# The first three up chunks split during the out-projections, and chunk 5 by seven products

## The chip, the cores and the metric

The kernel runs as one program on 1 core of a Trainium2 chip. The metric is the device time of one execution in microseconds; the median of the runs is compared. The profile is of one execution of its own.

## The reference

A trunk of two residual layers on x of 512 tokens by 1024 features, float32. Layer 0 mixes tokens with a gated linear attention (GLA), layer 1 with grouped-query softmax attention of 8 heads of 128. Each mixer ends with an out-projection, and a gated MLP follows it:

```python
def conv_ffn(h, w_up, w_conv, b_conv, w_down):
    u = h @ w_up                      # 1024 -> 2 x 2816
    u = conv(u) + b_conv              # width 3 along the tokens, per feature
    val, gate = jnp.split(u, 2, axis=-1)
    return (jax.nn.silu(gate) * val) @ w_down

for i in range(DEPTH):
    x = x + mixer_i(rmsnorm(x, norm_mix[i]))       # ends in "@ w_out"
    x = x + conv_ffn(rmsnorm(x, norm_ffn[i]), ...)
```

## The kernel before

**Numbers in two parts.** Each fp32 operand is split into a high part (fp32r, a copy that rounds) and a low part (the rest), and one fp32 product is three fp32r matmuls: high x high, high x low, low x high (`mm3`; L482 to L484 for a tile of 512 tokens). ScalarE makes the high part (L319), VectorE the low part by a subtraction (L320). Instead of that subtraction the low part can be made by a DMA: ScalarE writes the high part (L271) and its negative (L272), and a DMA from POOL's queue adds the full values onto that (`low_dma`, L308), from SBUF or from the weights in DRAM.

**Weights.** `Weights` holds a list of pieces to make, in the order of their use (`todo`). A piece of 128 x 1024 is loaded by SyncE into one of 5 buffers of the tag raw, then made into a high and a low part in buffers of the tags wh and wl (4 each); within the FFN every third piece goes into pairs of the tag x. `piece` makes what is asked for, then makes pieces ahead until the count given is ready, and starts the loads of the next ones. Larger buffers of the tag g (22) hold temporaries of all kinds (`big`).

**The up projection.** The 2816 features of u are 22 chunks of 128, each for val and gate. A chunk is done in one of two ways. The plain way (`plain_up`, L1041) takes two weight pieces of one layout and does 2 halves x 8 k-tiles x 3 = 48 matmuls of 128x512. The other (`seven_up`, L1083) is a scheme of Strassen's kind: seven products of half the size in place of eight, with sums of quarters of the weights (`summed`, L275: L283, L286, L293, L294) and of the inputs (`prepare_input`, L1164: differences of quarters, L1168 to L1171). It does 7 products x 4 pairs x 3 = 84 matmuls of 128x256 (L1074). ScalarE copies partial results between the products (L1095, L1102, L1129), and VectorE adds one pair (L1132). `SEVEN` lists the chunks done so, and the host lays their weights out by quarters. The first product of a chunk of sevens runs between the halves of the chunk before it. Of the pieces of sevens, those in `LOW_0` take the DMA for the low part of their first sum.

After either way come a convolution (L1117 on ScalarE, L1118 and L1119 on VectorE), silu and the product of the two halves (L1121, L1122). From chunk 9 on the down projection runs between up chunks.

**The inputs.** For the chunks 0 to 2 (below `SWITCH`) the matmuls read x times the norm's weight (xhl), and the result is multiplied by the tokens' factor R (L1062). Meanwhile `rescale` (L1029) makes four tiles xr of the fully normalised input, each of two k-tiles (L1035), with high parts nh on ScalarE and low parts nl by DMA; the chunks from 3 on read those. `prepare_input` changes the four xr in place into the differences, and makes the parts xt from them, again with the DMA. `INPUT_AT` says after which chunk this is done for which tile.

**Out-projections.** `out_steps` gives them as steps, each for one k-tile of one group of output features. In layer 0 (GLA) 8 steps run early, and the rest after the last two heads' tails. In layer 1 (attention) the twelve steps of `O_STEPS` run between the last heads' blocks, and the rest at the end. Heads end on TensorE with po (probabilities times v, L482 to L484), which reads pth (L1454, ScalarE) and ptl (L1455, VectorE); then oT is made from po (L1336 on ScalarE, L1337 on VectorE), and the out-projection's op (L535) reads it.

**What sets the order.** Instructions of an engine run in program order, which the scheduler of the language makes from the order of the code, the buffers and the dependencies. The engines meet through semaphores, and each queue of DMAs goes in order.

Of the kernel before, what the change touches and what calls it, by code (L numbers as in the profile page):

```python
# [9 lines left out]
F32R = mybir.dt.float32r  # L10
# [39 lines left out]
OUT_FIRST = 8  # L50
# [8 lines left out]
O_STEPS = (20, 22, 24, 27, 30, 33, 34, 34, 35, 35, 36, 37)  # L59
# [7 lines left out]
DOWN_AFTER = {9: 0, 17: 1}  # L67


SEVEN = (6, 7, 8, 10, 11, 12, 13, 15, 16, 18, 19, 20, 21)  # L70
UPA = 3
PA = 4
LOADS = 3
SWITCH = 3
INPUT_AT = {2: (0, 1), 3: (2,), 4: (3,)}
Q_DMA = ()
UP_DMA = (1, 2, 5)
LOW_0 = (7, 8)
LOW_1 = ()
LOW_2 = ()  # L80
STRIP_0 = ()
# [8 lines left out]
UPAW = 3  # L90
# [10 lines left out]
def hybrid_encoder_kernel(  # L101
# [39 lines left out]
    def bank(tag, n):  # L141
        return pp.tile([P, S], F32, tag=tag, bufs=PS[tag], name=nm(n))

    def pair(tag, bufs, dt, n):
        return sp.tile([P, 2 * S], dt, tag=tag, bufs=bufs, name=nm(n))

    def big(dt, n):
        return pair("g", 22, dt, n)
# [27 lines left out]
    class Weights:  # L176
# [68 lines left out]
        def make(self, key):  # L245
            src, i, h = key
            if i < 0:
                self.made[id(src), i, h] = self.make_vg(src, -i, h)
                return
            self.load(key)  # L250
            if (id(src), i) in self.sums:
                self.made[id(src), i, h] = self.summed(src, i, h)
                return
            r = self.loaded.pop((id(src), i, h))
            hi, lo = self.two()
            if any(src is a and i < n for a, n in self.by_dma):
                self.low_dma(hi, lo, r)
            elif any(src is a and i in UP_DMA for a in up):
                self.low_dma(hi, lo, r, src[i, :, h * 2 * S : (h + 1) * 2 * S].bitcast(F32R))
            else:  # L260
                self.split(hi, lo, r, 2 if src is w_first else 1, src is w_first and i == 0 and h == 0)
            self.made[id(src), i, h] = (hi, lo)
# [12 lines left out]
        def summed(self, src, i, h):  # L275
# [20 lines left out]
            r = self.strip[id(src), i][h]  # L296
            low = (LOW_0, LOW_1, LOW_2) if any(src is a for a in up) else (STRIP_0, (), STRIP_2)
            if i in low[h]:
# [41 lines left out]
    W = Weights()  # L340
    up = [w_up[i] for i in range(2)]
    down_w = [w_down[i] for i in range(2)]

    def add_up(layer, chunks):
        for m in chunks:
            W.add(up[layer], (m,), 4 if m in SEVEN else 2)
            if m in SEVEN and m - 1 not in SEVEN and m - 1 not in DOWN_AFTER:
                W.todo[-5:-3] = W.todo[-4], W.todo[-5]
# [137 lines left out]
    def feature_steps(wh, wl, hl, ps):  # L486

        for k in range(KC):
            sl = slice(k * P, (k + 1) * P)
            last = mm3(ps, wh[:, sl], wl[:, sl], *hl[k], k == 0, k == KC - 1)  # L490
            if k == 2:
                W.flush()
            yield last

    def feature_tile(*a):
        for last in feature_steps(*a):
            pass
        return last
# [20 lines left out]
    def out_steps(src, hl, nxt, late, order=(0, 1)):  # L519
# [20 lines left out]
        def end(ng):  # L540
            for n in range(2):
                c = ng * 2 + n
                dve.tensor_tensor(x[c], x[c], pss[ng][n], ALU.add)
                nxt.chunk(c)
            x_save(ng, order[0])
# [6 lines left out]
        for ng in (2, 3):  # L552
            yield from part(ng, [k for ks in late for k in ks])
            end(ng)


    def gla(norm, nxt):
        norm.high(0)
# [367 lines left out]
        def tail(h, last=None):  # L926

            t3 = gr.pop(h)
            for c in range(2):
                tp = bank("pt", "tp")  # L930
                for s in range(NT):
                    with tc.issue_after(last.ins) if last else ExitStack():
                        pe.transpose(tp[:, s * P : (s + 1) * P].bitcast(F32R),
                                     t3[:, s * DV + c * P : s * DV + (c + 1) * P], identr)
                t = big(F32R, "oT") if h >= 2 else pair("xhl", 8, F32R, "oT")
                w = prm[:, PC_GN + c : PC_GN + c + 1]
                act.activation(t[:, :S], tp, AF.Copy, scale=w)  # L937
                dve.scalar_tensor_tensor(t[:, S:], tp, w, t[:, :S].bitcast(F32), ALU.mult, ALU.subtract)
                oh[2 * h + c] = (t[:, :S], t[:, S:])
# [66 lines left out]
        osteps = out_steps(w_gout, oh, nxt, ((4, 5, 6, 7), (0, 1), (2, 3)), (1, 0))  # L1006
# [2 lines left out]
        sync.dma_start(cw, conv)  # L1009
        tail(0)  # L1010
        tail(1)
        for _ in osteps:
            pass
        return cw


    def ffn(layer, norm, cw, nxt):
        w_dn = down_w[layer]

        ahead = {(m + i // 2, i % 2): n for m in DOWN_AFTER for i, n in ((-1, 2), (0, 2), (1, 5))}  # L1020
        ahead.update({(m - 1 + i // 2, i % 2): n for m in SEVEN for i, n in ((-1, 2), (0, 2), (1, 5))})
        plain = {}
# [4 lines left out]
        scaled, fresh = [], []  # L1027
# [13 lines left out]
        def plain_up(m):  # L1041

            pss = []
            for t in range(2):
                ps = bank("s" if t else "acc", "up")
                feature_tile(*W.half(up[layer], 2 * m + t, max(UPAW if W.wide else UPA, ahead.get((m, t), 1))), norm.hl if m < SWITCH else fresh, ps)
                pss.append(ps)
                if t == 0 and m not in DOWN_AFTER:
                    begin_up(m + 1)
                if t == 0 and m in DOWN_AFTER:  # L1050
                    down.append(down_part(DOWN_AFTER[m], m))
                    next(down[-1])
                if m == 0 and t == 0:
                    norm.tokens()
                elif m == 0:
                    norm.rows()
                    rescale()
            for t, ps in enumerate(pss):
                u = ps
                if m < SWITCH:  # L1060
                    u = tmp("u", "u")
                    dve.tensor_tensor(u, ps, norm.R, ALU.mult)  # L1062
                yield t, u
# [14 lines left out]
        def begin_up(m):  # L1078
            if m in SEVEN:
                begun.append(seven_up(m))  # L1080
# [29 lines left out]
        def act_up(m):  # L1110

            res = {}
            for t, u in begun.pop(0) if m in SEVEN else plain_up(m):
                cc = ((layer * 2 + t) * FC + m) * 4
# [122 lines left out]
        for m in range(FC):  # L1237
# [5 lines left out]
            held.append(act_up(m))  # L1243
            for p in INPUT_AT.get(m, ()):
                prepare_input(p)
# [7 lines left out]
            else:  # L1253
                for i, y in enumerate(held):
                    t = big(F32R, "gu")
# [15 lines left out]
    def attention(norm, nxt):  # L1271
# [67 lines left out]
        def whole(gen):  # L1339
            while True:  # L1340
                try:
                    next(gen)
                except StopIteration as e:
                    return e.value
# [44 lines left out]
        ps = [bank("acc" if j < 2 else "pt", "av") for j in range(NT)]  # L1389
# [81 lines left out]
        osteps = out_steps(w_aout, oh, nxt, (range(5), (5,), (6,), (7,)))  # L1471
# [8 lines left out]
        for t in range(len(blocks) + LAG2):  # L1480
# [12 lines left out]
                turn(h, j // 2)  # L1493
            if 1 <= t <= len(blocks):
                copy(*blocks[t - 1])
        whole(osteps)

    norms = [Norm(i) for i in range(4)]
    cw = gla(norms[0], norms[1])
# [5 lines left out]
def _layout(inputs):  # L1505
# [61 lines left out]
    seven = np.stack(quarters, 1).transpose(0, 4, 3, 1, 2, 5).reshape(2, FC, P, 4 * S)  # L1567
    a["w_up"][:, list(SEVEN)] = seven[:, list(SEVEN)]
    dn = i["ffn_w_down"].reshape(2, FC, P, KC, P)
# [29 lines left out]
```

## Time and profile before

| | |
|---|---|
| median of 3 runs | 1087.22 us (1086.87 to 1087.8) |
| span of the profiled execution | 1085.5 us |
| TensorE busy (matmuls) | 1077.5 us, 99% of the span |
| VectorE busy | 888.5 us, 82% |
| ScalarE busy | 721.1 us, 66% |
| POOL busy | 136.7 us, 13% |
| DMA moved | 164.52 MB, mean 152 GB/s |
| TensorE clock granted | 1.00 throughout the stages named below |

The profile is of one execution with a span of 1085.5 us; the median of the timed runs is 1.7 us above it. Its times count from the start of the span. PE is TensorE, DVE VectorE, ACT ScalarE, SP SyncE. L numbers are lines of the kernel before; in the changed kernel they stand 5 to 10 lines lower. The out-projection of layer 0 ends near 218 us, the one of layer 1 near 736 us, and the FFN starts stand behind these.

### The profile page before, as it was taken

Reading aid. Unit: us, or ns where it says so; the run is one execution under the profiler, and the core shown is the slowest. Engines: PE = TensorE matmul, PEld = TensorE weight load, DVE = VectorE, ACT = ScalarE, POOL = GpSimd, SP = SyncE. Lnnn points to the kernel's source line nnn. Section 1 sums busy time; section 2 is a strip of 40 time slices with the busy share of each in tenths; the row PEclk is TensorE's granted clock in tenths of the full one; section 3 lists DMA queues with packets and bytes.
Section 4 is the critical chain, followed back from the end, with each engine's and each line's share of the span. In section 5 each row is a group of like instructions: output and inputs, shape, how many; then the busy total and the mean of one; then the engine's idle time right before and its main releaser. Section 6 shows DMA issues by size and latency. Waiting matters only on the chain.

```text
span 1085.5 us, 17391 instructions
## 1 busy us (share of the span) xinstructions
PE 1077.5 (99%) x6672; PEld 966.4 (89%) x6672; DVE 888.5 (82%) x1327; ACT 721.1 (66%) x1134; POOL 136.7 (13%) x153
## 2 busy tenths in 40 slices
PE   9999999999999999999999999999999999999998
PEld 8888988888999999999988888888889999999997
DVE  7998967569898899988755588666989889998882
ACT  8679575478775676666574677656877567666660
POOL 0212112021001100010015333002110010001000
PEclk9999999999999999999999999999999999999999
DMA  8744446499545633274767475549863473227542
GB/s 301 187 126 106 122 141 215 154 207 204 127 125 127 145 120 111 77 177 121 252 149 162 127 204 164 164 158 202 206 148 124 105 166 116 100 80 157 136 175 78
DMA packets 55763, 164.52 MB, mean 152 GB/s; under 512 B 6528, under 2 KB 7040, under 8 KB 55680
## 3 DMA queue, kind: packets, MB, share of 16 engines
q1 hardware_dynamic: 36192, 112.66, 32.2%
q0 software_dynamic: 14592, 42.21, 21.7%
q10 hardware_dynamic: 4896, 8.55, 2.1%
q8 instruction: 52, 0.85, 0.3%
q14 instruction: 31, 0.25, 0.1%
HBM read 114.89 MB, written 14.68 MB: 119 GB/s over the span
## 4 chain that ended last, share of the span: by engine, by line
PE 87%; DVE 6%; ACT 3%; DMA 2%; issue 2%; POOL 0%; SPq 0%; DVEq 0%; ACTq 0%; POOLq 0%
PE r L1074 37%; PE op L535 8%; PE vg L652 7%; PE up L482 4%; PE up L483 4%; PE up L484 4%; PE dn L483 2%; PE dn L484 2%; PE dn L482 2%; PE av L509 1%; PE A L482 1%; DVE wl L320 1%; PE A L484 1%; DMA nl<-xr 1%; PE B L484 1%
## 5 line engine op out<-in xcount | busy, mean ns | idle before, releaser
L320 DVE TENSOR_TENSOR wl<-raw,wh 128x1024 fp32r<-128x1024 f32 x156 | 189.8, 1220 | 31.3 <-ACT wh L319 31.1
L319 ACT ACTIVATE wh<-raw 128x1024 fp32r<-128x1024 f32 x156 | 162.6, 1053 | 73.4 <-PE op L535 20.7
L1074 PE MATMUL r<-gu,wh 128*128 128x256 f32 x896 | 161.2, 282 | 0.0
L1074 PE MATMUL r<-xt,wh 128*128 128x256 f32 x832 | 151.1, 283 | 0.4 <-ACT r L1095 0.3
L1074 PEld LDWEIGHTS r<-gu,wh 128*128 128x128 f32 x896 | 139.3, 190 | 1.0 <-ACT r L1211 0.2
L1074 PEld LDWEIGHTS r<-xt,wh 128*128 128x128 f32 x832 | 129.2, 190 | 1.6 <-ACT r L1095 1.1
L1074 PE MATMUL r<-gu,wl 128*128 128x256 f32 x448 | 126.3, 283 | 0.0
L1074 PE MATMUL r<-xt,wl 128*128 128x256 f32 x416 | 117.2, 283 | 0.0
L1074 PE MATMUL r<-nh,wh 128*128 128x256 f32 x312 | 88.8, 285 | 0.3 <-ACT r L1102 0.3
L1074 PE MATMUL r<-nh,wl 128*128 128x256 f32 x312 | 88.2, 283 | 0.0
L1074 PE MATMUL r<-nl,wh 128*128 128x256 f32 x312 | 87.9, 282 | 0.0
L1074 PEld LDWEIGHTS r<-gu,wl 128*128 128x128 f32 x448 | 85.1, 190 | 0.0
L1074 PEld LDWEIGHTS r<-xt,wl 128*128 128x128 f32 x416 | 79.1, 190 | 0.0
L482 PE MATMUL up<-nh,wh 128*128 128x512 f32 x192 | 75.3, 392 | 0.0
L483 PE MATMUL up<-nl,wh 128*128 128x512 f32 x192 | 75.2, 392 | 0.0
L484 PE MATMUL up<-nh,wl 128*128 128x512 f32 x192 | 75.2, 392 | 0.0
L535 PE MATMUL op<-oT,wh 128*128 128x512 f32 x256 | 72.4, 393 | 0.0
L271 ACT ACTIVATE wh<-raw 128x1024 fp32r<-128x1024 f32 x36 | 38.0, 1056 | 38.2 <-PE up L483 11.5
L1074 PEld LDWEIGHTS r<-nh,wh 128*128 128x128 f32 x312 | 59.3, 190 | 2.9 <-ACT r L1102 2.6
L1074 PEld LDWEIGHTS r<-nl,wh 128*128 128x128 f32 x312 | 59.4, 190 | 0.2
L1074 PEld LDWEIGHTS r<-nh,wl 128*128 128x128 f32 x312 | 59.4, 190 | 0.0
L535 PEld LDWEIGHTS op<-oT,wh 128*128 128x128 f32 x256 | 47.4, 188 | 9.7 <-ACT oT L937 0.3
(299 smaller groups left out, 2761.6 us busy)
## 6 DMA issues: line engine op xcount, KB each, us to landing
raw<-in_w_up_dram SPq DMA_DIRECT2D x84, 512.0 KB, 4.6
raw<-in_w_down_dram SPq DMA_DIRECT2D x44, 512.0 KB, 3.7
wl<-raw POOLq DMA_DIRECT2D x20, 512.0 KB, 5.3
wl<-in_w_up_dram POOLq DMA_DIRECT2D x16, 512.0 KB, 7.8
ring<-p ACTq DMA_DIRECT2D x32, 256.0 KB, 2.6
xw<-in_xw_dram SPq DMA_DIRECT2D x8, 512.0 KB, 6.6
raw<-in_w_v_dram SPq DMA_DIRECT2D x8, 512.0 KB, 5.9
raw<-in_w_g_dram SPq DMA_DIRECT2D x8, 512.0 KB, 4.0
```

The costliest lines, as they stand in the source:

```text
L271: act.activation(hi, r, AF.Copy)
L319: act.activation(hi[:, sl], a, AF.Copy)
L320: dve.tensor_tensor(lo[:, sl], a, hi[:, sl].bitcast(F32), ALU.subtract)
L482: mm(ps, wh, mh, start=start, stop=False)
L483: mm(ps, wh, ml, start=False, stop=False)
L484: return mm(ps, wl, mh, start=False, stop=stop)
L509: mm(ps[j][:, :width], hl[k][i == 2][:, j * P : (j + 1) * P], (wl if i == 1 else wh)[:, sl], start=k == 0 and i == 0, stop=k == KC - 1 and ...
L535: mm(pss[ng][n], wt[:, sl], mv, start=k == late[0][0] and i == 0, stop=k == late[-1][-1] and i == 2)
L652: last = mm(ps[j], m[:, js], w[:, sl], start=i in (1, 7, 2) and p == 0 and a == 0, stop=i in (4, 2, 3) and p == 3 and a == 2, skip_group_c ...
L1074: mm(dst, w[:, sl], m, start=start and j == 0 and a == 0, stop=j == len(pairs) - 1 and a == 2, skip_group_check=True)
```

## The change

The weights of the up chunks 0 to 2 of both layers are made during the remaining steps of the out-projection before them, one piece at each step in `EARLY_AT`, into buffers of the tag g. All six are split by ScalarE and VectorE. The low parts of the chunks 3 and 4 come by DMA from DRAM, where those of 1, 2 and 5 did. Chunk 5 becomes a chunk of sevens, and its first sum and that of chunk 6 have their low part by DMA too. The inputs of the sevens are all prepared after the chunks 2 and 3.

```diff
-SEVEN = (6, 7, 8, 10, 11, 12, 13, 15, 16, 18, 19, 20, 21)
+SEVEN = (5, 6, 7, 8, 10, 11, 12, 13, 15, 16, 18, 19, 20, 21)
+EARLY = 3
+EARLY_AT = (16, 17, 18, 20, 22, 24, 26, 28)
-INPUT_AT = {2: (0, 1), 3: (2,), 4: (3,)}
+INPUT_AT = {2: (0, 1), 3: (2, 3)}
-UP_DMA = (1, 2, 5)
-LOW_0 = (7, 8)
+UP_DMA = (3, 4)
+LOW_0 = (5, 6, 7, 8)
...
             r = self.loaded.pop((id(src), i, h))
-            hi, lo = self.two()
+            if i < EARLY and any(src is a for a in up):
+                hi, lo = big(F32R, "wh"), big(F32R, "wl")
+            else:
+                hi, lo = self.two()
...
+    def early(osteps, first):
+
+        for n, _ in enumerate(osteps, first):
+            if n in EARLY_AT:
+                W.ahead(1)
...
-        for _ in osteps:
-            pass
+        early(osteps, OUT_FIRST)
...
-                feature_tile(*W.half(up[layer], 2 * m + t, max(UPAW if W.wide else UPA, ahead.get((m, t), 1))), norm.hl if m < SWITCH else fresh, ps)
+                feature_tile(*W.half(up[layer], 2 * m + t, max(2 * EARLY if m < EARLY else UPAW if W.wide else UPA, ahead.get((m, t), 1))), norm.hl if m < SWITCH else fresh, ps)
...
-        whole(osteps)
+        early(osteps, len(O_STEPS))
```

Two places show what moves. The first is the end of attention in layer 1, on ScalarE. Before, from the split ahead of the last oT but one (raw1379 holds weights of the out-projection):

```order
L319 ACTIVATE wh1407_7471<-raw1289_7025 128x1024
L1336 ACTIVATE oT1410_7496<-po1400_7428 128x512
L1454 ACTIVATE pth1401_7447<-pt1411_7499 128x2x256
L1454 ACTIVATE pth1403_7449<-pt1412_7506 128x2x256
L319 ACTIVATE wh1433_7596<-raw1379_7339 128x1024
L1336 ACTIVATE oT1414_7532<-po1413_7519 128x512
```

And after (raw1443, raw1446 and raw1449 hold the first three pieces of the up weights, raw1297 and raw1387 weights of the out-projection):

```order
L324 ACTIVATE wh1415_7527<-raw1297_7081 128x1024
L324 ACTIVATE wh1450_7691<-raw1443_7656 128x1024
L1346 ACTIVATE oT1418_7552<-po1408_7484 128x512
L1464 ACTIVATE pth1409_7503<-pt1419_7555 128x2x256
L1464 ACTIVATE pth1411_7505<-pt1420_7562 128x2x256
L324 ACTIVATE wh1441_7652<-raw1387_7395 128x1024
L324 ACTIVATE wh1453_7710<-raw1446_7669 128x1024
L324 ACTIVATE wh1456_7728<-raw1449_7682 128x1024
L1346 ACTIVATE oT1422_7588<-po1421_7575 128x512
```

One split of up weights now stands ahead of the last oT but one and the pth behind it, and two more ahead of the last oT.

The second place is the FFN start of layer 1, on VectorE. Before, from the making of the fourth tile xr (L1035) to the first difference of the first tile (L1168):

```order
L1035 SCALAR_TENSOR_TENSOR xr1484_7870<-x942_5452,prm_66,R1474_7847 128x512 x2
L1119 SCALAR_TENSOR_TENSOR y1490_7885<-u1489_7883,cw_145,y1490_7885 128x511
L1118 SCALAR_TENSOR_TENSOR y1500_7960<-u1499_7958,cw_145,y1500_7960 128x511
L1062 TENSOR_TENSOR u1501_7964<-up1495_7927,R1474_7847 128x512
L1119 SCALAR_TENSOR_TENSOR y1500_7960<-u1499_7958,cw_145,y1500_7960 128x511
L320 TENSOR_TENSOR wl1510_7991<-raw1472_7815,wh1509_7990 128x1024
L1168 TENSOR_TENSOR xr1475_7849<-xr1475_7849 128x256
```

And after, where L1045 makes a tile and L1178 is that difference:

```order
L1045 SCALAR_TENSOR_TENSOR xr1499_7938<-x949_5507,prm_66,R1492_7922 128x512 x2
L1128 SCALAR_TENSOR_TENSOR y1508_7960<-u1507_7958,cw_145,y1508_7960 128x511
L1178 TENSOR_TENSOR xr1493_7924<-xr1493_7924 128x256
L1129 SCALAR_TENSOR_TENSOR y1508_7960<-u1507_7958,cw_145,y1508_7960 128x511
L1045 SCALAR_TENSOR_TENSOR xr1502_7945<-x950_5508,prm_66,R1492_7922 128x512 x2
```

The first difference of the first tile (xr1475 before, xr1493 after) now stands ahead of the making of the fourth.

## The prediction

> **What bounds the kernel now.** I read the page first, then the waits of TensorE, the chain that ended last, and the stretches of the FFN starts.
>
> ```profile
> span 1085.5 us, 17391 instructions
> PE 1077.5 (99%) x6672; PEld 966.4 (89%) x6672; DVE 888.5 (82%) x1327; ACT 721.1 (66%) x1134; POOL 136.7 (13%) x153
> PE 87%; DVE 6%; ACT 3%; DMA 2%; issue 2%; POOL 0%; SPq 0%; DVEq 0%; ACTq 0%; POOLq 0%
> ```
>
> TensorE is busy for 99% of the span and holds 87% of the chain. Matmuls overlap, so a TensorE that looks busy may still have lost time, and I look for its waits (columns: us in total, times, longest us).
>
> ```profile
> PE r L1074 <- ACT r L1102: 0.3, 1, 0.3
> PE r L1074 <- ACT r L1095: 0.3, 1, 0.3
> ```
>
> These are the only waits of the seven products that the view lists. So the time is the number of matmuls times their pace. The pace comes from long pieces of the chain (start, us, what, count), not from the mean durations of the groups:
>
> ```profile
> 187.83 30.26 PE op L535 x133
> 847.23 76.13 PE r L1074 x636
> L1074 PE MATMUL r<-xt,wh 128*128 128x256 f32 x832 | 151.1, 283 | 0.4 <-ACT r L1095 0.3
> L482 PE MATMUL up<-nh,wh 128*128 128x512 f32 x192 | 75.3, 392 | 0.0
> ```
>
> A 512-column matmul costs 30.26/133 = 0.2275 us, a 256-column one 76.13/636 = 0.1197 us. The durations, 392 and 283 ns, contain the overlap with the next one.
>
> VectorE is the second engine. In the FFN start of layer 1 it fills whole stretches (busy us of PE, PEld, DVE, ACT and POOL, then the granted clock, DMA share, GB/s):
>
> ```profile
> 769.80:781.00 11.20, 11.20 (x50) 9.17 (x49) 11.20 (x23) 10.23 (x15) 2.36 (x3) 1.00 0.80 186
> 781.00:792.00 11.00, 11.00 (x50) 9.00 (x49) 11.00 (x22) 7.52 (x11) 1.97 (x3) 1.00 0.97 196
> 815.00:840.00 25.00, 24.30 (x177) 22.50 (x176) 24.58 (x35) 17.71 (x26) 0.00 (x0) 1.00 0.38 127
> ```
>
> TensorE shows a hole only in 815 to 840, where it is busy for 24.30 of 25.00. The chain through that hole:
>
> ```profile
> 819.98 2.28 DVE wl L320 x2
> 822.27 3.56 DMA raw<-in_w_up_dram
> 826.20 0.91 ACT wh L319
> 827.16 1.46 ACT y L1117 x2
> 828.95 3.14 PE r L1074 x24
> ```
>
> VectorE frees a raw buffer late, so a load starts late; ScalarE stands at the split of that load, and a copy that TensorE needs stands behind it.
>
> **The change, part by part.** The profiled span is 1085.5 us and the median of the runs 1087.22, so 1.7 us lie outside the span. I sum changes of the span and add them to the median.
>
> *Chunk 5 by seven products.* Per layer 48 matmuls of 512 columns go and 84 of 256 come; the order of TensorE is longer by just 2 x 36 rows and otherwise unchanged, so the change does what it says. By the paces 48 x 0.2275 = 10.92 and 84 x 0.1197 = 10.05, so −0.87 us per layer, −1.7 us in both, all of it on the path. By the mean durations it would be 48 x 0.392 = 18.8 against 84 x 0.283 = 23.8, that is slower; but those overlap.
>
> [...]
>
> *Splits and sums.* Counted off the order between the copy of R and the first convolution of chunk 9, VectorE has in each layer three 128x1024 splits fewer (seven of the chunks 0, 3, 4 and 6 among them go, two of chunk 5 come, and what is made ahead shifts) and one more each of L283, L286 and L1132, all 128x512.
>
> ```profile
> L320 DVE TENSOR_TENSOR wl<-raw,wh 128x1024 fp32r<-128x1024 f32 x156 | 189.8, 1220 | 31.3 <-ACT wh L319 31.1
> L319 ACT ACTIVATE wh<-raw 128x1024 fp32r<-128x1024 f32 x156 | 162.6, 1053 | 73.4 <-PE op L535 20.7
> L283 DVE TENSOR_TENSOR raw<-raw 128x512 f32<-128x512 f32 x3 | 2.1, 687 | 0.0
> ```
>
> That is −3 x 1.22 + 3 x 0.69 = −1.6 us of VectorE, in a stretch in which TensorE gets 0.87 us shorter: VectorE gains some 0.7 us on it. The hole is 25.00 − 24.30 = 0.7 us. I take half of it as gone, −0.4. Bounds: −0.7 if VectorE is then early enough; +1.4, twice the hole again, if four sevens in a row (chunks 5 to 8) exhaust what was made ahead where three nearly did. The splits that moved into the out-projections cost nothing there but by their place:
>
> *The end of attention in layer 1.* The rows of ScalarE in the section on the change show the place: oT is a head's scaled output, pth and ptl are the parts of the transposed probabilities, and raw1443, raw1446 and raw1449 the first three pieces of the up weights. One up split moved ahead of the last oT but one, two ahead of the last; VectorE has their low parts at the same places. What waits for that, in the trace of before, with the landing time of such loads:
>
> ```profile
> 699.72 8.80 SPq L230 DMA_DIRECT2D raw<-in_w_up_dram  x6
> 703.92 0.60 ACT L1336 ACTIVATE oT<-po 128x512 fp32r<-128x512 f32 x1 [2.49 <-PE po L484]
> 705.16 1.28 DVE L1455 TENSOR_TENSOR ptl<-pt,pth 128x512 fp32r<-128x512 f32 x2
> 706.03 0.40 PE L483 MATMUL po<-ptl,vh 128*128 128x512 f32 x1
> 709.38 0.69 DVE L1337 TENSOR_TENSOR oT<-po,oT 128x512 fp32r<-128x512 f32 x1 [1.68 <-ACT oT L1336]
> 711.27 1.07 PE L535 MATMUL op<-oT,wh 128*128 128x512 f32 x4
> raw<-in_w_up_dram SPq DMA_DIRECT2D x8, 256.0 KB, 3.3
> raw<-in_w_up_dram SPq DMA_DIRECT2D x84, 512.0 KB, 4.6
> ```
>
> The first up piece comes in two halves and lands near 699.72 + 0.4 + 3.3 = 703.4, half a microsecond before the oT. Its split holds ScalarE for 1.05 us, to 704.5, and then its low part holds VectorE for 1.22 us ahead of the ptl that TensorE reads at 706.03. The ptl of before starts 0.87 us ahead of that matmul, so 1.1 us has no slack: TensorE waits about 1.0 us. The third piece waits for a buffer; SyncE issues its six loads over 8.80 us there, and I put this one 6 us after the first: it lands near 705.8 + 4.6 = 710.4, and after its split and the two steps of oT (1.05, 0.60, 0.69, overlapping a little) the last oT is there at about 712.5, against a need at 711.27 + 1.0 = 712.3. I take +1.0 for the place. Bounds: 0, if the piece lands 1 us earlier and falls into the 2.49 us that ScalarE idles there, and +2.5, if the third load takes 6 us.
>
> At the end of the GLA's out-projection two splits go ahead of the last oT as well:
>
> ```profile
> 187.77 1.58 DVE L938 SCALAR_TENSOR_TENSOR oT<-tp,prm,oT 128x512 fp32r<-128x512 f32 x2 [0.76 <-ACT oT L937]
> 191.86 1.07 PE L535 MATMUL op<-oT,wh 128*128 128x512 f32 x4
> ```
>
> That oT is done at 189.35 and first read at 191.86; 2.5 us cover the 1.1 to 2.2. I take 0, bounds 0 and +0.5.
>
> *Inputs of the sevens, one chunk earlier.* Each scaled tile (xr) gives its low part by a DMA into nl, becomes differences (L1168 to L1171), and goes by a DMA from POOL into xt. As VectorE's rows of layer 1 in that section show, the first difference of tile 0 moved ahead of the making of tile 3, and it overwrites an xr that the DMA into nl still reads.
>
> ```profile
> 753.01 0.86 POOL L308 DMA_DIRECT2D nl<-xr  x1 [2.29 <-DVE xr L1035]
> 756.01 9.13 DMA nl<-xr
> 762.40 0.86 POOL L308 DMA_DIRECT2D nl<-xr  x1 [2.69 <-DVE y L1119]
> 774.23 0.39 PE L483 MATMUL up<-nl,wh 128*128 128x512 f32 x1
> 792.24 0.41 DVE L1171 TENSOR_TENSOR xr<-xr 128x256 f32<-128x256 f32 x1
> 795.65 0.86 POOL L308 DMA_DIRECT2D xt<-xr  x1 [6.77 <-ACT xt L272]
> L1074 PE MATMUL r<-xt,wh x36: 278/283/315, 804.3 to 814.9; 128*128 128x256 f32 x36
> DMA to landing us min/median/max: 4.5/5.3/7.9
> ```
>
> So VectorE stands until about 753.0 + 9.1 = 762.1, then makes tile 3; its nl is issued at about 766 where it was at 762.40, lands at 775 by the same 9.1, and is read at 774.23 (+1.0, the wait in attention, shifts both). That is up to 0.8 us late; two loads that moved ahead leave the DMA queues freer, so I take +0.3, bounds 0 and +1.5. The differences of tile 3 come after 12 us less of VectorE's work than before (instructions counted off the order from the copy of R on, at their groups' durations), some 4 of which go to the wait: done near 784 instead of 792.2, issued near 787.5, landed by 5.3 near 793, or 795.4 by 7.9. Chunk 5 reads tile 3 a plain chunk, 10.9 us, ahead of the 804.3 + 1.1 of now: 794.5. I take 0, bounds 0 and +3. Layer 0's order makes all four tiles first: 0.
>
> The sum: −1.7 − 0.4 + 1.0 + 0.3 = −0.8, so 1087.2 − 0.8 = 1086.4 us.
>
> **Rivals.** What a measurement of this kernel can tell from no change is about 0.2%, 2.2 us: faster is below 1085.0, slower above 1089.4.
>
> *A, the new waits don't come.* The piece lands before ScalarE is free, nl lands in time, the hole goes: −1.7 − 0.7 = −2.4. Layer 0 has a smaller hole, seen only in the pace of its first sevens:
>
> ```profile
> 286.56 26.29 PE r L1074 x216
> ```
>
> That is 26.29/216 = 0.1217 us, 216 x 0.002 = 0.4 us above the other piece's pace; without it −2.8, 1084.4. For it speak ScalarE's 2.49 us of idle at the oT and the loads moved out of the busiest stretch; against it that ptl has no slack.
>
> *B, slower: chunk 5's inputs land late in layer 1.* It decides when tile 3's xt lands after 794.5. If only half of the 8 us is won, it is issued at 791.6, lands at 796.9 to 799.5, 2.4 to 5.0 late; with 3.7 of that, +1.0 in attention, +0.3, and no hole filled, it is −1.7 + 5.0 = +3.3: 1090.5. For it: VectorE was full from 769.8 to 792 and now waits first. Against it: the order has far less ahead of tile 3.
>
> *C, a pace that doesn't halve.* If each matmul had a large fixed part, the seven products would gain nothing from 10.92/84 = 0.130 us on, and with the durations for paces they would cost 23.8 − 18.8 = 5.0 us a layer: 1087.2 + 10.0 + 0.9 = 1098.1. The rows give a fixed part of 2 x 0.1197 − 0.2275 = 0.012 us, and 636 matmuls in one piece stand behind it. [...]
>
> **How the numbers follow.** The forecast, a change within 0.2%, 0.45, and its own range is 1085.0 to 1089.0. A 0.36, B 0.18, C 0.01. Faster 0.36, within 0.2% 0.45, slower 0.19. The range reaches to 1083.4, A and a microsecond for holes too short for the list of waits, and to 1090.0, the nearer part of B.
>
> **What would show it.** Of the changed kernel: TensorE's paces stay at 0.2275 and 0.1197, and r of chunk 5 runs in 10 us. A wait of PE po (L488) on ptl of about 1 us near 706, and none at the last oT above 0.5. VectorE's L1178 waiting on the DMA into nl for about 4 us near 758. No wait of chunk 5's r on a DMA into xt: one of 2 us or more there is B. No wait at po and none in 815 to 840 is A. I am wrong in kind if TensorE loses time where I put none: in layer 0, or past chunk 9.

## The result and the profile after

The changed kernel takes 1094.28 us (median of 5 runs, 1093.28 to 1095.71) against 1086.87 us before (5 runs, 1086.5 to 1087.8). The ratio is 1.007, 95% interval 1.0057 to 1.0082: 7.4 us slower. The profiled execution has a span of 1092.9 us, 7.4 more than before.

The page after, the same three lines as before:

```profile
span 1092.9 us, 17553 instructions
PE 1078.8 (99%) x6744; PEld 969.7 (89%) x6744; DVE 898.1 (82%) x1339; ACT 727.8 (67%) x1146; POOL 136.7 (13%) x153
PE 83%; DVE 7%; DMA 4%; ACT 3%; issue 2%; POOL 0%; SPq 0%; DVEq 0%; ACTq 0%; POOLq 0%
```

TensorE is still busy for 99%, and that number hides the loss. Its share of the chain fell from 87% to 83%, and DMAs rose from 2% to 4%: now and then it waits. Its waits after of 0.5 us and more that before doesn't have, or has shorter (us in total, times, longest us; line numbers here and below are those of the kernel that is spoken of):

```profile
PE r L1084 <- ACT r L1105: 3.2, 1, 3.2
PE op L540 <- DVE x L548: 0.7, 1, 0.7
PE r L1084 <- ACT r L1112: 0.7, 1, 0.7
PE up L488 <- DVE xhl L457: 0.6, 2, 0.3
PE po L487 <- DVE oT L1347: 0.5, 1, 0.5
PE up L487 <- ACT xhl L452: 0.5, 1, 0.5
```

The waits in the list come to 6.2 us. To find all of the loss I went through the trace matmul by matmul and summed the time from one start to the next above the pace (0.227 us for 512 columns, 0.1196 for 256), by place. "FFN start" is the 130 us behind an out-projection; its first 20 us hold the norm.

| us over the pace | out-projection 0 | FFN start 0 | end of attention and out-projection 1 | norm 1 | rest of FFN start 1 |
|---|---|---|---|---|---|
| before | 0.6 | 1.0 | 2.0 | 0.2 | 2.3 |
| after | 1.6 | 7.5 | 3.2 | 2.1 | 0.4 |
| change | +1.0 | +6.4 | +1.2 | +1.9 | −1.9 |

With −1.7 us for the matmuls that is +6.9 of the 7.4 us; the rest is spread over the span.

**The big loss: chunk 5 of layer 0.** Its products in the chain (start, us, what), then VectorE and ScalarE ahead of them in the timeline, with the idle time before an instruction and what ended it in brackets:

```profile
282.88 11.81 PE r L1084 x84
```

```profile
249.69 0.42 DVE L1178 TENSOR_TENSOR xr<-xr 128x256 f32<-128x256 f32 x1
254.04 0.43 DVE L1178 TENSOR_TENSOR xr<-xr 128x256 f32<-128x256 f32 x1 [3.93 <-DMA nl<-xr]
...
279.59 0.68 DVE L288 TENSOR_TENSOR raw<-raw 128x512 f32<-128x512 f32 x1
280.31 0.63 ACT L290 ACTIVATE wh<-raw 128x512 fp32r<-128x512 f32 x1 [1.78 <-DVE raw L288]
280.85 0.76 ACT L1127 ACTIVATE y<-up,cw 128x512 f32<-128x512 f32 x1
281.51 1.04 ACT L276 ACTIVATE wh<-raw 128x1024 fp32r<-128x1024 f32 x1
282.45 0.37 ACT L1105 ACTIVATE r<-r 128x256 f32<-128x256 f32 x1
```

Read it from the bottom. TensorE waits for a copy of 0.37 us (L1105). ScalarE has it behind L290 and L276, pieces of weights for later, and L1127, a convolution; L290 waited for VectorE's L288; and VectorE had stood for 3.93 us at the last input tile's difference, until the DMA that reads that tile into nl had landed. From 254.0 to 279.4 VectorE is busy for 24.3 of 25.4 us and doesn't make it up. Little of this work is late for its own reader: TensorE's longest wait for a piece of weights is 0.4 us. It is late for what stands behind it.

Then a second price. Stretches of 2 us (PE, PEld, DVE, ACT, POOL busy, granted clock, DMA share, GB/s):

```profile
281.00:283.00 2.00, 0.12 (x1) 0.12 (x2) 1.32 (x2) 2.00 (x4) 0.00 (x0) 1.00 0.00 0
283.00:285.00 2.00, 2.00 (x11) 2.00 (x12) 0.83 (x2) 1.80 (x3) 0.87 (x1) 0.54 0.03 8
285.00:287.00 2.00, 2.00 (x13) 2.00 (x13) 0.53 (x2) 1.06 (x1) 0.00 (x0) 0.61 0.59 80
287.00:289.00 2.00, 2.00 (x19) 2.00 (x18) 1.43 (x2) 0.70 (x2) 0.00 (x0) 1.00 1.00 188
```

After the pause the granted clock is 0.54 and 0.61 for 4 us, with 11 and 13 matmuls in 2 us where there are 19 at full clock. The 84 products of chunk 5 take 11.81 us, 0.1406 each, against 84 x 0.1197 = 10.05: another 1.8 us. The pause here is 3.36 us long; sevens_alone below shows the same behind one of 2.0 us.

**The norm of layer 1.** ScalarE, then VectorE:

```profile
740.15 1.06 ACT L276 ACTIVATE wh<-raw 128x1024 fp32r<-128x1024 f32 x1 [3.93 <-DMA raw<-in_w_up_dram]
742.06 1.32 ACT L452 ACTIVATE xhl<-x,prm 128x512 fp32r<-128x512 f32 x2
746.36 1.07 ACT L276 ACTIVATE wh<-raw 128x1024 fp32r<-128x1024 f32 x1 [2.97 <-DMA raw<-in_w_up_dram]
748.27 0.71 ACT L452 ACTIVATE xhl<-x,prm 128x512 fp32r<-128x512 f32 x1
743.83 1.23 DVE L298 TENSOR_TENSOR sum<-raw,raw 128x1024 f32<-128x1024 f32 x1 [6.61 <-DMA raw<-in_w_up_dram]
```

Both engines stand for loads of the chunks 4 and 5, with the xhl that TensorE reads next behind them. Before, the L271 there waited for a buffer that TensorE freed:

```profile
730.05 1.06 ACT L271 ACTIVATE wh<-raw 128x1024 fp32r<-128x1024 f32 x1 [3.20 <-PE op L535]
```

Now it has a buffer, comes earlier, and waits for the load. In 735 to 750 the DMA share is 1.03.

**What got better.** The hole in layer 1 is gone; the stretch that shows it, 7 us later than before:

```profile
822.00:847.00 25.00, 25.00 (x192) 24.00 (x191) 24.79 (x36) 18.32 (x28) 0.00 (x0) 1.00 0.50 142
```

### The profile page after: what moved, and what is told of

It is laid out like the page before. It is cut to its first block, busy times and chain, and to the rows that moved or that the text cites. A ratio compares the mean times of both kernels' runs of the same rounds, so it can differ in the third digit from the quotient of the medians.

```text
span 1092.9 us, 17553 instructions
## 1 busy us (share of the span) xinstructions
PE 1078.8 (99%) x6744; PEld 969.7 (89%) x6744; DVE 898.1 (82%) x1339; ACT 727.8 (67%) x1146; POOL 136.7 (13%) x153
## 4 chain that ended last, share of the span: by engine, by line
PE 83%; DVE 7%; DMA 4%; ACT 3%; issue 2%; POOL 0%; SPq 0%; DVEq 0%; ACTq 0%; POOLq 0%
PE r L1084 39%; PE vg L663 7%; PE up L488 4%; PE up L487 4%; PE up L489 4%; PE op L540 4%; DMA raw<-in_w_up_dram 2%; PE dn L487 2%; PE dn L488 2%; PE dn L489 2%; DVE wl L325 2%; PE av L514 1%; PE A L487 1%; PE A L489 1%; PE B L487 1%
## 5 line engine op out<-in xcount | busy, mean ns | idle before, releaser
L324 ACT ACTIVATE wh<-raw 128x1024 fp32r<-128x1024 f32 x156 | 162.1, 1052 | 61.5 <-DVE raw L299 11.0
L1084 PE MATMUL r<-xt,wh 128*128 128x256 f32 x896 | 164.0, 284 | 3.6 <-ACT r L1105 3.2
L1084 PEld LDWEIGHTS r<-xt,wh 128*128 128x128 f32 x896 | 140.4, 192 | 4.7 <-ACT r L1105 3.6
L1084 PE MATMUL r<-xt,wl 128*128 128x256 f32 x448 | 127.0, 284 | 0.0
L1084 PEld LDWEIGHTS r<-xt,wl 128*128 128x128 f32 x448 | 85.9, 192 | 0.0
L487 PE MATMUL up<-nh,wh 128*128 128x512 f32 x160 | 62.6, 392 | 0.0
L488 PE MATMUL up<-nl,wh 128*128 128x512 f32 x160 | 62.6, 392 | 0.0
L489 PE MATMUL up<-nh,wl 128*128 128x512 f32 x160 | 62.6, 391 | 0.0
L298 DVE TENSOR_TENSOR sum<-raw,raw 128x1024 f32<-128x1024 f32 x44 | 53.6, 1218 | 9.9 <-DMA raw<-in_w_up_dram 9.9
L325 DVE TENSOR_TENSOR wl<-sum,wh 128x1024 fp32r<-128x1024 f32 x44 | 53.7, 1220 | 6.2 <-ACT wh L324 6.1
```

The lines of the kernel that those rows point to most:

```text
L298: dve.tensor_tensor(both(e), both(a21).to_broadcast([P, 2, S]), both(t1), ALU.subtract)
L324: act.activation(hi[:, sl], a, AF.Copy)
L325: dve.tensor_tensor(lo[:, sl], a, hi[:, sl].bitcast(F32), ALU.subtract)
L487: mm(ps, wh, mh, start=start, stop=False)
L488: mm(ps, wh, ml, start=False, stop=False)
L489: return mm(ps, wl, mh, start=False, stop=stop)
```

## The experiments

Theory 1: an engine that stands for a DMA at the head of its queue, the wait for nl above all, starves TensorE. Theory 2: four chunks of sevens in a row are too much for VectorE. Theory 3: the early splits do the harm. All runs are compared with the kernel before in the same job (1086.9 to 1087.4 us). The table of the losses by place, as above, for the runs. The losses are those of the one execution that was profiled; its own time stands in the last column, and where it is far from the median (chunk5_only, conv_and_heads, nl_and_heads) the losses are not those of a typical execution:

| us over the pace | out-proj. 0 | FFN start 0 | attention, out-proj. 1 | norm 1 | rest 1 | median us | profiled us |
|---|---|---|---|---|---|---|---|
| chunk5_only | 0.6 | 7.1 | 2.0 | 0.2 | 5.4 | 1093.15 | 1095.79 |
| early_only | 1.5 | 9.5 | 3.7 | 7.7 | 1.5 | 1104.71 | 1106.37 |
| input_behind_conv | 1.3 | 2.5 | 3.5 | 1.8 | 0.4 | 1090.04 | 1089.06 |
| norm_first | 1.5 | 8.2 | 3.2 | 0.2 | 4.5 | 1098.11 | 1097.75 |
| both_orders | 1.6 | 4.2 | 3.4 | 0.2 | 5.7 | 1095.42 | 1094.57 |
| heads_first | 1.0 | 4.1 | 2.3 | 0.2 | 6.1 | 1094.79 | 1093.81 |
| conv_and_heads | 1.4 | 2.5 | 2.6 | 4.0 | 0.4 | 1093.30 | 1090.77 |
| nl_by_vector | 1.4 | 9.9 | 3.3 | 2.2 | 4.8 | 1100.57 | 1101.4 |
| nl_and_heads | 1.6 | 11.7 | 2.4 | 8.0 | 5.8 | 1106.41 | 1110.14 |
| new_buffer | 1.4 | 2.1 | 3.2 | 2.2 | 8.1 | 1097.42 | 1097.39 |
| new_buffer_orders | 0.9 | 2.1 | 2.3 | 0.2 | 7.2 | 1093.35 | 1092.49 |
| early_orders | 1.4 | 1.6 | 2.7 | 0.2 | 3.2 | 1090.13 | 1090.15 |
| sevens_alone | 0.6 | 9.1 | 2.0 | 0.2 | 6.9 | 1098.76 | 1098.54 |
| inputs_in_before | 0.6 | 1.2 | 2.2 | 0.2 | 1.0 | 1086.83 | 1087.04 |
| inputs_again, the same kernel | 0.6 | 1.3 | 2.1 | 0.2 | 1.4 | 1087.15 | 1087.23 |

The last two rows are one kernel in two executions; so differences of some 0.4 us are scatter.

**One part alone: chunk5_only.**

```diff
-EARLY = 3
-EARLY_AT = (16, 17, 18, 20, 22, 24, 26, 28)
+EARLY = 0
+EARLY_AT = ()
```

> The changed kernel without the early splits: no piece of the up weights is made during the out-projections on purpose, chunk 5 stays one of seven products. Theory 1 (layer 0 loses its 6.5 us because VectorE stands for 3.9 us in L1178 until the DMA into nl has landed, now that all inputs are prepared after chunk 3): the wait and the loss at TensorE in chunk 5 of layer 0 stay, the losses at the end of both out-projections and in the norm of layer 1 (1.0, 1.8 and 1.9 us) go, about 1089 to 1090. Theory 2 (four chunks of sevens in a row simply need more of VectorE than there is): the same, or worse, since the splits of chunks 1 and 2 come back into the FFN start: 1090 to 1094. Theory 3 (the early splits and their loads do the harm, also in the FFN): 1085 to 1086.

1093.15 us, ratio 1.0059 (1.0044 to 1.0074). The low parts of the chunks 3 and 4 still come by DMA here. The losses at the out-projections and in the norm went, as both first theories said, and theory 3 is out as the whole cause. But the loss in the FFN has another face:

```profile
PE up L489 <- DMA wl<-in_w_up_dram: 4.6, 3, 2.5
PE r L1084 <- DMA wl<-in_w_up_dram: 2.3, 2, 1.9
```

Without the splits made ahead, low parts by DMA land late, for plain chunks (up) and for sevens (r). Neither theory had that. VectorE's wait for nl in layer 0, which theory 1 expected to stay, is down to 1.85 us. The three executions that weren't profiled took 1092.85 to 1093.28 us, so the table's row, of one of 1095.79, is some 2.6 us too much for this kernel.

**The other part alone: early_only.**

```diff
-SEVEN = (5, 6, 7, 8, 10, 11, 12, 13, 15, 16, 18, 19, 20, 21)
-INPUT_AT = {2: (0, 1), 3: (2, 3)}
-UP_DMA = (3, 4)
-LOW_0 = (5, 6, 7, 8)
+SEVEN = (6, 7, 8, 10, 11, 12, 13, 15, 16, 18, 19, 20, 21)
+INPUT_AT = {2: (0, 1), 3: (2,), 4: (3,)}
+UP_DMA = (3, 4, 5)
+LOW_0 = (7, 8)
```

> The early splits alone: chunk 5 goes back to the plain way with its low parts by DMA, the inputs are prepared as before; low parts of chunks 3 and 4 by DMA as changed. Theories 1 and 2: the 6.5 us of layer 0 go and the 1.7 us of saved matmuls too, the 1.0, 1.8 and 1.9 us at the out-projections and the norm stay: 1089 to 1091.5. Theory 3: 1094 to 1096.

1104.71 us, ratio 1.0157 (1.014 to 1.0174): slower than the whole change, and by none of the theories' numbers. Both norms lose, 6.4 (of the 9.5 in the table) and 7.7 us. VectorE in layer 0, and TensorE's clock behind it:

```profile
224.32 1.23 DVE L298 TENSOR_TENSOR sum<-raw,raw 128x1024 f32<-128x1024 f32 x1 [4.22 <-DMA raw<-in_w_up_dram]
225.47 0.74 DVE L457 SCALAR_TENSOR_TENSOR xhl<-x,prm,xhl 128x512 fp32r<-128x512 f32 x1
```

```profile
224.00:226.00 2.00, 0.00 (x0) 0.00 (x0) 1.68 (x2) 0.00 (x0) 0.00 (x0) 1.00 1.11 326
228.00:230.00 2.00, 2.00 (x11) 1.87 (x9) 0.68 (x2) 0.00 (x0) 0.00 (x0) 0.50 0.09 24
```

It is the mechanism of theory 1 at another place and with another DMA: the sum of a later chunk of sevens waits for its load ahead of the norm's xhl. TensorE stands, and then runs at a granted clock of 0.50. Behind the norm, VectorE stands for nl in layer 0 here too, for 6.2 us, though the inputs are prepared as in the kernel before.

**The wait moved by an order: input_behind_conv.** conv[m] is the last convolution step of chunk m on VectorE.

```diff
-                prepare_input(p)
+                with tc.issue_after(conv[2].ins) if p == 3 else ExitStack():
+                    prepare_input(p)
```

> The changed kernel with one order more: the differences of the last input tile stand behind the convolution of chunk 2 on VectorE, so VectorE does that work while the DMA into nl lands. Theory 1: the wait of 3.9 us in L1178 shrinks to under 0.5 us, TensorE's wait of 3.2 us in chunk 5 of layer 0 goes, and the granted clock stays at 1.00 there; about 1088 (6 us less). Theory 2: VectorE has the same work, and TensorE waits at the same place or one chunk later, 1092 to 1095.

1090.04 us, ratio 1.0024 (1.0015 to 1.0034): 4.2 us less than the change, 6 expected. VectorE's wait of 3.93 us in layer 0 is gone; the only one for nl that is left stands in layer 1, at 762.41, and the change had it there too. Layer 0's stretch runs through at full clock:

```profile
DVE xr L1179 <- DMA nl<-xr: 0.5, 1, 0.5
```

```profile
280.00:290.00 10.00, 10.00 (x86) 10.00 (x85) 7.95 (x11) 5.66 (x10) 0.53 (x1) 1.00 0.64 157
```

Same work, another order, and 5.0 of the 6.4 us in FFN start 0 are gone. 1.5 us stay, most of them at 303 to 305, where VectorE is full (9.9 of 10 us from 300 to 310) and where the change has them too: theory 2 has that share.

**The norm: norm_first.** What is made of the up weights after the early pieces stands behind the norm's last xhl, on ScalarE and VectorE.

```diff
         def make(self, key):
+            with ExitStack() as held:
+                for ins in self.behind:
+                    held.enter_context(tc.issue_after(ins))
+                self.make_now(key)
...
+        W.behind = norm.on_act, norm.on_dve
         held = []
         for m in range(FC):
...
             held.append(act_up(m))
+            W.behind = ()
```

> The changed kernel with one order more: everything made by ScalarE and VectorE for pieces of the up weights after the early ones stands behind the last xhl of the norm. If TensorE's 1.9 us lost in the up matmuls of chunk 0 in layer 1 come from ScalarE (3.9 and 3.0 us in L276) and VectorE (6.6 us in L298) standing for late loads ahead of xhl, they go: 1094.3 - 1.9 = 1092.4, and layer 0's out-projection is as it was. If the loads themselves are late for all (DMA share over 1.0 from 735 to 750), the loss only moves behind the norm: 1094 or more.

1098.11 us, ratio 1.0099 (1.0084 to 1.0114). The norm's loss went, 2.1 to 0.2, so its cause is shown. But the total rose by 3.8: layer 1 now has layer 0's loss, by the same wait, and the same clock.

```profile
771.00 0.43 DVE L1185 TENSOR_TENSOR xr<-xr 128x256 f32<-128x256 f32 x1 [4.43 <-DMA nl<-xr]
```

```profile
806.00:808.00 2.00, 0.00 (x0) 0.00 (x0) 2.00 (x3) 1.83 (x5) 0.00 (x0) 1.00 0.03 6
810.00:812.00 2.00, 2.00 (x11) 2.00 (x11) 0.69 (x1) 2.00 (x3) 0.00 (x0) 0.50 0.58 207
```

**Orders together: both_orders, heads_first, conv_and_heads.** The first two add to input_behind_conv the order on the norm, and then the order of layer 1's early splits behind the last oT; the third has the order on the last tile and the one on the heads, without the norm's.

```diff
-                split(pos[h], t)
+                parts = split(pos[h], t)
+                if h == QH - 1:
+                    W.behind = parts
```

> The changed kernel with both added orders: the last input tile's differences behind chunk 2's convolution, and all pieces made after the early ones behind the last xhl of the norm. Theory 1 (an engine that stands for a DMA at the head of its queue starves TensorE; the waits are for nl and for raw loads, and the four sevens in a row are not too much work): VectorE waits for nl by less than 0.5 us in both layers, the 1.9 us in the norm of layer 1 go and do not come back in chunk 5, 1090.0 - 1.9 = 1088.1. Rival (the loads of the chunks 3 to 5 are late for everybody, so an order only moves the loss): TensorE loses 2 to 4 us behind the norm or in chunk 5 of layer 1, 1090 to 1093.

> The same with a third order: the early splits of layer 1 stand behind the last head's oT on ScalarE and VectorE. If the early splits ahead of the last heads' steps cost what the end of attention lost (3.24 us over the pace in the changed kernel, 1.99 before), it goes: 1.2 us below the kernel with both orders, 1086.9. If that loss is of something else, or the splits are then late for the norm: no less than there, 1088.

> The changed kernel with the last tile's differences behind chunk 2's convolution (1090.0) and the early splits of layer 1 behind the last head's oT, without the order on the norm, whose price was late inputs (TensorE waited 3.3 us for the DMA into xt in layer 1). Theory 1, with each loss at its own place: 1090.0 - 1.7 = 1088.3. If the orders are not additive, the freed engines run into the next DMA: 1090 or more.

Measured 1095.42 (1.0077, 1.0062 to 1.0092), 1094.79 (1.0071, 1.0055 to 1.0087) and 1093.30 us (1.0056, 1.004 to 1.0073). Each order does its own part: the norm's loss goes with the first, and attention's falls from 3.4 to 2.3 with the second. None of the sums came out. In both_orders the first of TensorE's waits, and VectorE's for nl, are now

```profile
PE r L1092 <- DMA xt<-xr: 3.3, 1, 3.3
DVE xr L1186 <- DMA nl<-xr: 6.5, 2, 4.5
```

and in conv_and_heads the norm pays 4.0 instead of 1.8, 1.7 of it by a stretch from 747.18 on where a 512-column matmul takes 0.43 us in place of 0.23; its profiled execution was 2.5 us under the median. My reading is that each relief lets something else arrive earlier at a queue's head. The rows show it for nl in both_orders; for the others it isn't shown.

**No DMA for nl: nl_by_vector, nl_and_heads.**

```diff
-                W.low_dma(hi, lo, xr)
+                W.split(hi, lo, xr)
```

> The changed kernel with the low parts nl by a subtraction on VectorE in place of the DMA: four more instructions of 1.2 us per layer on VectorE, and nothing of it waits for a DMA any more in L1178. Theory 1 (the wait for the landing of nl set the loss of layer 0): VectorE's 3.9 us of standing go against 4.9 us of work, which comes earlier; TensorE's wait of 3.2 us in chunk 5 of layer 0 shrinks to under 1 us and the clock stays at 1.00: 1089 to 1091. Theory 2 (too much work for VectorE in the four sevens): 1 us more work than there was waiting makes it worse, 1095 or more.

> The same, with the early splits of layer 1 behind the last head's oT. That order alone took 1.1 us at the end of attention and 0.6 us at the out-projection of layer 0 between the kernels with two and three orders: 1.5 us below the kernel with nl on VectorE. If the order only delays the splits and the norm pays: the same time as there.

1100.57 us (1.0124, 1.0109 to 1.0139) and, with the order on the heads, 1106.41 us (1.0178, 1.0161 to 1.0195). This is theory 2's number: with 4.9 us more of work per layer on VectorE, the differences come late, and TensorE waits for what hangs on them.

```profile
PE r L1084 <- DMA xt<-xr: 5.6, 2, 3.0
PE r L1084 <- DMA wl<-in_w_up_dram: 2.8, 1, 2.8
```

So a VectorE that stands is bad, and one with four more instructions is worse: there is no spare VectorE time ahead of chunk 5.

**The wait without its reason: new_buffer, new_buffer_orders.** The differences go into a tile z of their own.

```diff
-            dve.tensor_tensor(b11, b12, b11, ALU.subtract)
+            dve.tensor_tensor(c11, b12, b11, ALU.subtract)
...
+            y = z
```

> The changed kernel with the differences of the input tiles written into a buffer of their own, so they need not wait for the DMA that reads the tile; the work is the same. If the wait for nl is the cause in layer 0: VectorE's 3.9 us in L1178 go, TensorE's 3.36 us in chunk 5 and the 1.6 us of slow clock behind it go, 1094.3 - 5 = 1089. If VectorE's amount of work is the cause: TensorE loses 3 us or more at chunk 5 or 6 all the same, 1092 to 1095. If the freed VectorE only runs into the next transfer (buffers of the tag g, xt landing): the wait has another name, 1092 or more.

> The same with the pieces made after the early ones behind the norm's last xhl, and layer 1's early splits behind the last oT. If the losses are additive: 1.9 and 1.7 us less than with the new buffer alone, 1085.5 if that comes out at 1089. If they hang together by VectorE and the transfers: no better than 1089, with TensorE waiting for a DMA into xt or wl in layer 1.

In layer 0 the theory holds: VectorE has no wait for nl any more, and FFN start 0 falls from 7.5 to 2.1 with the same amount of work and nothing moved by hand. In layer 1 the new buffer changed VectorE's order: the first difference starts at 781.2, where the change has it at 768.2, and the inputs came late. In the list of TensorE's waits (us in total, times, longest) that is:

```profile
PE r L1084 <- DMA xt<-xr: 4.6, 2, 4.3
```

The total is 1097.42 us (1.0098, 1.0083 to 1.0113), and with the orders on norm and heads 1093.35 (1.006, 1.0043 to 1.0077).

**The early splits with the orders: early_orders.** Chunk 5 plain as in early_only, with the orders of heads_first on norm and heads.

> The early splits alone, chunk 5 the plain way with low parts by DMA as in the earlier run of them, but with the pieces after them behind the norm's last xhl, and layer 1's splits behind the last oT. If the 6.4 and 7.7 us lost in the two norms came from VectorE and ScalarE standing for raw loads ahead of xhl, they go: 1104.7 - 14.1 = 1090.6, and some 1.7 less by the order at the heads, 1089. If loads are late for all, 1095 or more.

1090.13 us, ratio 1.003 (1.0018 to 1.0042), as expected: 14.6 us come from two orders. The splits made early, even so, don't pay: against the kernel before 0.8 us go at the out-projection of layer 0, 0.7 at the end of attention, and 0.6 and 0.9 in the two FFN starts.

**Chunk 5 without the rest: sevens_alone.** The early splits off as in chunk5_only, the order of input_behind_conv, and

```diff
-UP_DMA = (3, 4)
-LOW_0 = (5, 6, 7, 8)
+UP_DMA = (1, 2)
+LOW_0 = (5, 7, 8)
```

> The kernel before with chunk 5 by seven products and nothing else of the change: no early splits; low parts of the chunks 1 and 2 by DMA as before, of the first sums of 5, 7 and 8 too; the inputs as in the change with the last tile's differences behind chunk 2's convolution. Theory 1: without waits for DMAs at the head of a queue the sevens pay, 1087.2 - 1.7 = 1085.5. Theory 2: VectorE has one more chunk of sums in the same time and lacks the relief by the early splits, 2 us or more lost in each layer between chunks 5 and 9, 1089.5 or more.

1098.76 us, ratio 1.0106 (1.0091 to 1.0121): theory 2's side by the number. But TensorE waits for low parts by DMA more than for one by VectorE, and theory 2 says nothing of those:

```profile
PE up L489 <- DMA wl<-in_w_up_dram: 3.6, 1, 3.6
PE r L1085 <- DMA wl<-in_w_up_dram: 2.6, 1, 2.6
PE r L1085 <- DVE wl L325: 1.9, 1, 1.9
```

**The inputs alone: inputs_in_before, inputs_again, inputs_earlier.** The kernel before with `INPUT_AT = {2: (0, 1), 3: (2, 3)}`, the same with more rounds, and with `{2: (0, 1, 2), 3: (3,)}`.

> The kernel before with one edit: inputs prepared as in the change, tiles 2 and 3 both after chunk 3. Theory 1: the wait does not need chunk 5 by seven products; VectorE stands for nl for 3 to 4 us in at least one layer, and TensorE, which reads these inputs a chunk later than in the change, loses 0 to 2 us: 1087 to 1089. Theory 2 (four sevens in a row are what costs): no wait and no loss, 1087.2.

> The kernel before with the inputs prepared as in the change, once more and with more rounds. If the hole of layer 1's FFN start shrinks by it (25.00 - 24.30 us of TensorE before, 25.00 - 24.81 in the first run of this): 0.5 to 1 us below the kernel before, with an interval that leaves out no change. If the first run was scatter: within 0.05% of it.

> One step further: three input tiles after chunk 2, the last after chunk 3. If earlier inputs only relieve VectorE later on: the same as with two and two, or up to 0.5 us less. If VectorE then stands for the DMA into nl as in the changed kernel: 1 us or more slower than that.

No wait for nl in the first of them, against theory 1's number (1.1 us in the second, in layer 1, where the kernel before has 1.5): VectorE, which still had the splits of the chunks 3 and 4 to do there, reached the differences when nl had landed. 1086.83 us (0.9993, 0.9984 to 1.0003) looked like a gain; with more rounds it is 1087.15 (1.0, 0.9991 to 1.0009), and one step further 1087.33 (0.9999, 0.999 to 1.0008). So that was scatter.

**A pause by itself: pause_in_before.** The kernel before with copies that nobody reads ahead of a copy that chunk 12 waits for.

```diff
             r3 = bank("s", "r3")
+            for _ in range((16, 10)[layer] if m == 12 else 0):
+                act.activation(r3[:, H:], r2, AF.Copy)
             act.activation(r3[:, :H], r2, AF.Copy)
```

> The kernel before with idle copies on ScalarE ahead of the copy that chunk 12 of sevens waits for: 16 in layer 0 (some 4.5 us, of which 1.4 are hidden, so a pause of about 3 us), 10 in layer 1 (2.8 us, a pause of about 1.4). If the clock falls after an idle time of 2.3 us and more but not of 2.0 and less, as in the runs so far: in layer 0 the granted clock is near 0.5 for 3 to 4 us behind the pause and TensorE loses 1.2 to 1.6 us besides it, in layer 1 nothing besides the pause: 1087.2 + 3 + 1.4 + 1.4 = 1093. If a pause costs its own length alone: 1091.6.

1095.84 us, ratio 1.0086 (1.0071 to 1.0101). The edit missed its aim: the copies were spread among other work, so there was no long pause but several of at most 1.7 us. Behind them the clock stayed at 1.00, and the long pause was not tried this way. The limit that I had expected, a fall from 2.3 us on and none at 2.0, was already wrong by sevens_alone: there the clock fell behind a pause of 2.0 us.

No kernel here beats the kernel before.

## Why the prediction was wrong

**The matmuls, −1.7 us: right.** A long piece of products after, for the one of 76.13 us before:

```profile
855.28 75.90 PE r L1084 x636
```

That is 0.1193 us each, the pace that the step took.

**Splits and sums, −0.4 with bounds −0.7 and +1.4: too small in layer 1 (−1.9), and for layer 0 it had no term.** The 1.5 us that stay in layer 0 when the wait for nl is gone are about its upper bound. The step took the count of VectorE's work as its price. Less work, together with the earlier inputs, let VectorE come earlier to an instruction that waits for a DMA.

**The end of attention, +1.0: right in size (+1.2), and half right in kind.** ScalarE stood for the raw load ahead of oT and pth, as said:

```profile
710.91 1.06 ACT L324 ACTIVATE wh<-raw 128x1024 fp32r<-128x1024 f32 x1 [2.25 <-DMA raw<-in_w_up_dram]
711.88 0.58 ACT L1346 ACTIVATE oT<-po 128x512 fp32r<-128x512 f32 x1
```

But TensorE waited 0.5 us at po for the oT that frees its only bank, and not the 1.0 us for ptl that I had summed, so the size is partly luck. heads_first took 1.1 us of it away. For layer 0's out-projection 0 was wrong: it lost 1.0, and not at the oT, but at op, which waits for x (L548) behind a split on VectorE.

**"Layer 0's order makes all four tiles first: 0": this step failed.** The wait of about 4 us for nl was foreseen, with its line, but in layer 1, where it came to 0.5 us: I had taken 9.1 us for that DMA, as in the trace of before, and it landed after 4.5 to 4.8. In layer 0 the wait came to 3.93. The issue of the last nl of layer 0 on POOL:

```profile
246.44 0.86 POOL L313 DMA_DIRECT2D nl<-xr  x1 [1.03 <-ACT nl L277]
```

VectorE reached the last tile's difference right behind its neighbour's (249.69, above), near 250.1, and this DMA landed at 254.0, 7.6 us after its issue. The DMA is no slower than before: there the same one took 7.8 us and landed at 252.4, but VectorE came to that difference at 263.94:

```profile
263.94 0.43 DVE L1168 TENSOR_TENSOR xr<-xr 128x256 f32<-128x256 f32 x1
```

I had asked whether the differences stand behind the making of the tiles; what decides is whether they stand behind the landing. With the slow clock behind it, it cost 5.0 of the 6.4 us in FFN start 0, as input_behind_conv shows. A loss in layer 0 is what the prediction itself had named as the sign of being wrong in kind. Rival B's price came in both_orders and new_buffer (3.3 and 4.3 us for xt in layer 1), not in the change itself.

**What stood in no step:** the norm of layer 1 (+1.9), by loads that now find a buffer early and stand ahead of xhl; and the clock, 1.6 to 1.8 us behind the one long pause.

**What stays open.** The early splits lose 0.3 to 1.0 us in the out-projection of layer 0 in every order tried, and the 1.5 us that stay in FFN start 0 were put to VectorE's load by its full stretches, but no run took work away there. In chunk5_only, nl_by_vector and sevens_alone TensorE waited for low parts by DMA; no run changed only those DMAs, so their share stays open. Why the scheduler's order differs between the layers was not tried.

## What to carry to other kernels

Work taken off a full engine was not free time here: VectorE came sooner to an instruction that waits for a DMA (3.93 us at L1178 in layer 0), and all behind it waited too. Before moving work, list for each engine the first instruction that waits for a transfer, when that transfer lands, and who needs what stands behind it; the sum of durations doesn't show it. When everything has to be ready one chunk earlier, a saving of 0.87 us per layer in matmuls has to be set against the margins of every chain that feeds that chunk (here nl, differences, xt, low parts), not against the totals.

## What the runs showed of the hardware

The length of a pause alone doesn't decide whether the clock falls. Three pauses show it, in stretches of 3.41 us with the granted clock third from the end; first chunk5_only, in layer 0, a pause of 2.0 us from 303.7 on, behind which the clock stays at 1.00:

```profile
300.75:304.16 3.41, 3.06 (x26) 2.86 (x24) 3.41 (x7) 2.58 (x6) 0.00 (x0) 1.00 0.92 157
304.16:307.57 3.41, 1.90 (x16) 1.91 (x17) 3.38 (x6) 2.25 (x4) 0.00 (x0) 1.00 0.56 166
307.57:310.99 3.42, 3.42 (x31) 3.42 (x30) 3.42 (x5) 3.25 (x5) 0.00 (x0) 1.00 0.44 152
```

Then sevens_alone, in layer 0, a pause of the same 2.0 us, behind which the clock falls to 0.50:

```profile
282.68:286.09 3.41, 1.53 (x11) 1.15 (x10) 3.39 (x5) 3.41 (x7) 0.51 (x1) 1.00 0.00 0
286.09:289.50 3.41, 3.41 (x18) 3.41 (x17) 1.87 (x3) 1.22 (x2) 0.36 (x1) 0.50 0.84 172
```

And nl_by_vector, in layer 1, a pause of 3.1 us from 807.4 on, behind which the clock stays at 1.00:

```profile
805.87:809.29 3.42, 1.65 (x12) 1.36 (x11) 3.42 (x7) 3.31 (x5) 0.00 (x0) 1.00 1.02 238
809.29:812.70 3.41, 2.17 (x16) 1.96 (x16) 3.41 (x5) 0.59 (x2) 0.00 (x0) 1.00 0.94 202
```

What else decides is not shown: no run placed a long pause on purpose.

The slow stretch of the changed kernel is 3.41 us long, from 283.15 to 286.56, at a granted clock of 0.50. Its products start 0.213 us apart, against the pace of 0.1197, and the first 18 behind the pause take 3.75 us from start to start, against 18 x 0.1197 = 2.15: 1.6 us. In nl_by_vector and sevens_alone the 82 products from 307.71 and 305.72 on, with a slow stretch among them, take 11.50 and 11.57 us, and in chunk5_only 82 without one take 10.06: 1.4 and 1.5 us.

ScalarE and VectorE passed no waiting instruction at the waits shown here: behind L276 (3.93 and 2.97 us), L290 (1.78), L298 (6.61) and L1178 (3.93) all else stood, at L1178 also the product that starts at 254.38, which input_behind_conv ran at 249.74.
